# Last two experts: all rows summed, normed and stored without them, their lists' rows normed apart and written over

## The chip, the cores and the metric

The kernel runs on one core of one Trainium2 chip. A core has a matrix engine (PE), a vector engine (DVE), a scalar engine (ACT), GpSimd (POOL) and SyncE (SP), each with its own queue, worked off in order. SP, ACT and POOL also issue DMAs, which all run on the core's 16 DMA engines. The metric is the device time in microseconds of one execution, as the median of several runs.

## What is computed

One decoder block on 512 tokens of 1024 channels: a mixer (attention and a gated delta rule), then a mixture of experts, then a norm of each row. The change touches the last two. In the words of the reference:

```python
logits = xt @ w_router + b_router
top_v, top_e = top_k(logits, 4)            # 4 of 32 experts for each token
gates = softmax(top_v)
yb = clamped_swiglu(xb @ w1[e] + b1[e]) @ w2[e] + b2[e]
y[token] += yb * gate                      # over a token's four experts
x = x + gate2 * y
out = x * rsqrt(mean(x * x) + 1e-6) * final_norm_w
```

w1 of one expert is 1024 x 2048 and w2 is 1024 x 1024, both float32: 8 MB and 4 MB, 384 MB for all 32.

## The kernel before

The experts are run in an order by their number of tokens; `ROOM` (line 34) says how many tokens the list of each place can hold: 128, 96, 64 or 32, and so on. A list of 64 is one round whose rows are halves of a token (partitions 0 to 63 hold channels 0 to 511, the others the rest); one of 32 is a round of quarters; 96 is one of each. What does not fit goes through the loop at line 1481, which makes no turn with these inputs.

The steps (lines 1376 to 1379) go u0, u1, d0, u2, d1, ..., u31, d30, d31. Step "u" (`up`, line 1166) multiplies a list's rows by w1 and applies the activation (lines 1185 to 1187: ACT and DVE); step "d" (`down`, line 1190) multiplies by w2. Weights come in tiles of 1 MB, eight for a "u" and four for a "d", by SP's queue (lines 817 and 820), issued up to three steps ahead, into 15 buffers used in turn: six of the pool `late`, two of `wp` and seven of `moe` (`rawx`, line 800). A tile's buffer is free when PE has read it.

The DRAM tensor `yd` holds the rows so far: it starts as the mixer's output, and each round but the last scales its result by gates (line 1211, DVE) and adds it to `yd` by an indirect DMA that accumulates (line 1212, POOL). Such a DMA waits until the one before it has landed. The rows of a list are read from `h2d` by an indirect DMA (line 1156, POOL).

At the end (expert place 31, 64 tokens), `residual` (line 1219) loads the four blocks of 128 rows of `yd` once place 30 has been added; `gates_by_expert` and `bias2` make every token's share of the second bias with PE. `add_rows` (line 1247) brings the last list's result to its tokens by products with a matrix of zeros and ones, adds it to the blocks, norms each block (Square with a sum on ACT, the power -0.5 on POOL at line 1284, a scaling on DVE at lines 1297, 1300 and 1303) and stores it by SP (line 1307).

The order of each engine's queue is made when the program is built, by a planner that takes what it holds to be ready, the earlier in the program first; `in_order` fixes it in places. A weight load of SP's also waits until the eighth load before it has landed.

Of the kernel before, what the change touches and what calls it, by code (L numbers as in the profile page):

```python
# [14 lines left out]
OP = mybir.AluOpType  # L15
# [15 lines left out]

ROOM = [128, 128, 64, 64, 96, 64, 64, 192, 32, 96, 32, 160, 64, 64, 128, 64, 128, 64, 96, 64, 96, 64, 96, 64, 96, 64, 96, 64,
        32, 96, 32, 64]
# [9 lines left out]
def tile_block(ctx: ExitStack, tc, x, c, w_ada, b_ada, norm1_w, w_in, conv_w, A_log, dt_bias, dn_norm_w,  # L45
# [750 lines left out]
    E, HB, NR = 32, 64, 6  # L796
    NL, NM = 6, 7
    seq = [0]

    def rawx():  # L800
# [235 lines left out]
    def accumulator():  # L1036
        AL.append(ps2.tile([P, 512], F32, name="acc", bufs=6))
        return AL[-1]
# [148 lines left out]
            V.scalar_tensor_tensor(ut, sg, GATE_MAX, ut, op0=OP.min, op1=OP.mult)  # L1187
            UT[key] = ut

    def down(keys, rounds, tiles, ix, go, between=lambda i: None, last=False, first=False):  # L1190

        as_ = [AT.pop(c) for c in keys]
        accs = [accumulator() for _ in rounds]
# [10 lines left out]
                between(i)  # L1204
        for q, ((g, _), py) in enumerate(zip(rounds, accs)):
            if last:
                add_rows(py, go[:, q:q + 1], ix[:, q:q + 1], first)
# [11 lines left out]
    def residual():  # L1219

        for name, pool in (("res", moe), ("out", late)):
            ts = [pool.tile([P, 2048], F32, name="raw", bufs=NM if pool is moe else NL) for _ in range(2)]
            RES[name] = [ts[b // 2][:, b % 2 * D:b % 2 * D + D] for b in range(NTB)]
        for b in range(NTB):
            nc.sync.dma_start(RES["res"][b], yd[b * P:(b + 1) * P, :])
        RES["p2"] = [accumulator() for _ in range(2)]
        for n in range(2):
            bias2(RES["p2"][n], 1, n)

    def gates_by_expert():  # L1230

        g4 = late.tile([P, 2048], F32, name="raw", bufs=NL)[:, :NTB * 3 * E].rearrange("p (b a e) -> p b a e", b=NTB, a=3)
        for b in range(NTB):
            G.tensor_copy(g4[:, b], gt[:, 0, b, None, :].to_broadcast([P, 3, E]))
        gT = moe.tile([P, 2048], F32R, name="raw", bufs=NM)[:96, :T]
        pt = flat(ps2.tile([P, 4, P], F32, name="tr", bufs=2))[:96]
        for b in range(NTB):
            PE.transpose(pt[:, b * P:b * P + P], g4[:, b].rearrange("p a e -> p (a e)"), ident)
        S.copy(gT, pt)
        V.tensor_tensor(gT[64:], pt[64:], gT[64:].bitcast(F32), op=OP.subtract)  # L1240
        RES["g"] = gT

    def bias2(pn, b, n):

        PE.matmul(pn, RES["g"][:, b * P:b * P + P], b2s[:96, n * 512:n * 512 + 512], start=True, stop=False)

    def add_rows(py, gcol, ix, first):
# [8 lines left out]
        y = moe.tile([P, D], F32, name="ylast", tag="big")  # L1256
        yh, yl = (moe.tile([P, 512], F32R, name=n, tag="y", bufs=3) for n in ("yh", "yl"))
        V.scalar_tensor_tensor(y[:, :512], py, gcol, gate2s[2], op0=OP.mult, op1=OP.mult)
        S.copy(yh, y[:, :512])
        V.tensor_tensor(yl, y[:, :512], yh.bitcast(F32), op=OP.subtract)  # L1260
        of = lambda t, n: t[n * HB:n * HB + HB]
        ones_of = lambda b, n: one[n * HB:n * HB + HB, b]

        if not first:
            RES["p2"] = [accumulator() for _ in range(3)]
        others = [a for a in AL[-6:] if all(a is not q for q in RES["p2"][:2])]
        acc = [[flat(ps2.tile([P, 4, P], F32, name="tr", bufs=2)) for _ in range(2)], RES["p2"][:2], others[:2], others[2:]]
        fx = moe.tile([P, 3, 2 * NTB], F32, name="fx")
        cut = [slice(n * 512, n * 512 + 512) for n in range(2)]
        if first:  # L1270
            for b in (0, 2, 3):
                for n in range(2):
                    bias2(acc[b][n], b, n)
        for n in range(2):
            PE.matmul(acc[0][n], ident, RES["res"][0][:, cut[n]], start=not first, stop=False)

        def rms(b, xs):

            n = len(xs)
            sq, ms, sc = (fx[:, i, 2 * b:2 * b + n] for i in range(3))  # L1280
            for i, x in enumerate(xs):
                S.activation(y[:, :D // n], x, AF.Square, accum_out=sq[:, i:i + 1])
                S.activation(ms[:, i:i + 1], sq[:, i:i + 1], AF.Identity, scale=1.0 / D, bias=ms[:, 0:1] if i else epsc)
            G.tensor_tensor(sc[:, 0:1], ms[:, n - 1:n], mhalf[:, :1], op=OP.pow)

        with in_order(PE, V, S, G):
            for b in (1, 2, 3, 0):
                for n in range(2):
                    PE.matmul(acc[b][n], ones_of(b, n), of(yh, n), start=(b > 0 and not first), stop=False)
                    PE.matmul(acc[b][n], ones_of(b, n), of(yl, n), start=False, stop=True)  # L1290
                for a in {1: (1,), 3: (2, 3)}.get(b, ()):
                    for n in range(2):
                        V.tensor_tensor(RES["res"][a][:, cut[n]], RES["res"][a][:, cut[n]], acc[a][n], op=OP.add)
                if b == 1:
                    G.tensor_tensor(RES["out"][1], RES["res"][1], fnw, op=OP.mult)
                    rms(1, [RES["res"][1]])
            V.tensor_scalar(RES["out"][1], RES["out"][1], fx[:, 2, 2:3], None, op0=OP.mult)
            for b in (2, 3):
                rms(b, [RES["res"][b]])
                V.scalar_tensor_tensor(RES["out"][b], RES["res"][b], fx[:, 2, 2 * b:2 * b + 1], fnw, op0=OP.mult, op1=OP.mult)  # L1300
            rms(0, acc[0])
            for n in range(2):
                V.scalar_tensor_tensor(RES["out"][0][:, cut[n]], acc[0][n], fx[:, 2, 0:1], fnw[:, cut[n]], op0=OP.mult,
                                       op1=OP.mult)
                S.copy(RES["res"][0][:, cut[n]], acc[0][n])
        for b in (1, 2, 3, 0):
            nc.sync.dma_start(out[b * P:(b + 1) * P, :], RES["out"][b])


    for i, c in enumerate(COLS[1]):  # L1310
# [81 lines left out]
    for s, (what, i) in enumerate(steps):  # L1392
        while ahead < min(len(steps), s + 4):
            w_, j = steps[ahead]
            which, w_all = (1, w1) if w_ == "u" else (2, w2)
            load(which, j, weights(w_all, j), after=None if j > 1 else idx[0:1, 0:1].bitcast(F32))
            ahead += 1
        if what == "u" or i == E - 1:
            while pending:
                pending.pop(0)()  # L1400
        if what == "d":
            if i == E - 2:
                gates_by_expert()
            c0, c1 = COLS[i][0], COLS[i][-1] + 1
            down(COLS[i], ROUNDS[i], W.pop((2, i)), idx[:, c0:c1], gate[:, c0:c1], lambda _: pending and pending.pop(0)(),
                 i == E - 1, i == E - 1)
            if i == E - 2:
                residual()
            continue
        up(COLS[i], ROUNDS[i], W.pop((1, i)), sel_of(i))  # L1410
        for c in COLS[i]:
            pending.append(turn(AT, UT, "a", c))
        if i == 0:
# [67 lines left out]
    with tc.For_i(0, nrounds, 1):  # L1481
# [8 lines left out]
        down(["o"], [(2, 0)], W.pop((2, "o")), ix, go, last=True)  # L1490


def tables():
# [39 lines left out]
```

## Time and profile before

| | us |
|---|---|
| median of 3 runs (lowest, highest) | 1479.51 (1478.02, 1483.98) |
| the profiled execution's own time | 1475.38 |
| its span, first to last instruction | 1473.6 |
| busy: PE, DVE, ACT, POOL | 1377.2, 442.5, 270.3, 231.0 |
| read from HBM | 467.67 MB |

The expert stage is about the last 1000 us. Times below are microseconds from the start of the span. In a line of the timeline the first number is the start, the second the length; "x8" merges eight instructions; in brackets stands how long the engine sat idle before, and what ended that.

### The profile page before, as it was taken

What the parts mean: (1) busy time and instruction counts of PE and PEld (TensorE: products, weight loads), DVE (VectorE), ACT (ScalarE), POOL (GpSimd) and SP (SyncE); (2) the same over time, 40 slices, a digit from 0 to 9 for tenths busy, and PEclk for the clock granted to TensorE, in tenths of its full rate; (3) what the DMA queues carried; (4) which work ended last, traced back from release to release, by engine and by line L of the source; (5) the groups of instructions that cost most, each with busy time, mean ns of one, the idle gap of its engine ahead of it and who ended that gap; (6) DMA issues with size and microseconds to landing.
All of it is one profiled execution on the core that took longest, in us unless ns stands there. A gap on an engine that the chain in (4) does not pass through costs nothing.

```text
span 1473.6 us, 21094 instructions
## 1 busy us (share of the span) xinstructions
PE 1377.2 (93%) x8278; PEld 653.4 (44%) x8278; DVE 442.5 (30%) x1127; ACT 270.3 (18%) x595; POOL 231.0 (16%) x222
## 2 busy tenths in 40 slices
PE   5999898999899999999999999999999999988784
PEld 4777777779843333343333333333333333322131
DVE  3586985666781120201020220000211000100002
ACT  5554213573320000001010100000100001000002
POOL 0324105012321111110120120101111111100012
PEclk9999999999999999999999999999999999998798
DMA  9445465002689899999999999999999999999993
GB/s 342 148 143 163 149 204 166 29 13 82 282 333 346 322 387 414 406 412 413 410 404 410 417 405 413 411 406 408 417 409 407 416 411 415 410 410 411 419 384 137
DMA packets 100629, 482.11 MB, mean 327 GB/s; under 512 B 13112, under 2 KB 33240, under 8 KB 51376
## 3 DMA queue, kind: packets, MB, share of 16 engines
q1 hardware_dynamic: 88384, 459.54, 77.8%
q0 software_dynamic: 10960, 19.02, 5.4%
q10 hardware_dynamic: 1184, 2.18, 0.4%
q8 instruction: 66, 1.08, 0.3%
q14 instruction: 35, 0.29, 0.1%
HBM read 467.67 MB, written 17.44 MB: 329 GB/s over the span
## 4 chain that ended last, share of the span: by engine, by line
PE 56%; DMA 29%; DVE 9%; ACT 2%; issue 1%; POOL 1%; SPq 0%; ACTq 0%; POOLq 0%; DVEq 0%
PE acc L1178 27%; DMA raw<-in_w 24%; PE acc L1201 13%; PE tr L1148 2%; DVE macc L356 2%; DMA raw<-in_w_ada 2%; DVE wL L145 2%; DVE cv L313 1%; PE acc L1049 1%; PE ps L706 1%; DMA raw<-in_w_out 1%; PE mm L875 1%; PE mm L873 1%; PE mm L874 1%; POOL sn L327 1%
## 5 line engine op out<-in xcount | busy, mean ns | idle before, releaser
L1178 PE MATMUL acc<-raw,xS 128*64 128x512 f32 (+1 forms) x2944 | 575.2, 608 | 18.4 <-DMA raw<-in_w 18.3
L1178 PEld LDWEIGHTS acc<-raw,xS 128*64 128x64 f32 (+1 forms) x2944 | 173.3, 130 | 395.5 <-issue 331.2
L1201 PE MATMUL acc<-raw,aS 128*64 128x512 f32 (+1 forms) x1952 | 325.9, 515 | 9.9 <-DMA raw<-in_w 9.9
L1186 DVE TENSOR_SCALAR ut<-acc 128x512 f32<-128x512 f32 (+1 forms) x48 | 28.4, 616 | 526.2 <-PE acc L1178 477.1
L1201 PEld LDWEIGHTS acc<-raw,aS 128*64 128x64 f32 (+1 forms) x1952 | 98.7, 126 | 175.3 <-issue 134.7
L1185 ACT ACTIVATE sg<-acc 128x512 f32<-128x512 f32 (+1 forms) x48 | 24.4, 538 | 667.6 <-PE acc L1178 667.6
L1212 POOL DMA_INDIRECT yd<-y,idx x47 | 74.6, 1587 | 418.0 <-DVE y L1211 271.0
L1211 DVE SCALAR_TENSOR_TENSOR y<-acc,gate,gate 128x512 f32<-128x512 f32 (+1 forms) x47 | 30.3, 674 | 297.4 <-PE acc L1201 297.4
L1156 POOL DMA_INDIRECT xg<-h2d,idx x46 | 48.7, 1060 | 438.2 <-PE tr L1148 398.2
L284 PE MATMUL mm<-hH,wH 128*128 128x512 f32 x144 | 57.9, 402 | 2.4 <-ACT cu L310 2.3
L285 PE MATMUL mm<-hL,wH 128*128 128x512 f32 x144 | 57.4, 399 | 0.0
L286 PE MATMUL mm<-hH,wL 128*128 128x512 f32 x144 | 57.3, 398 | 0.0
L1149 ACT COPY xS<-tr 128x512 f32<-128x512 f32 (+1 forms) x46 | 24.1, 525 | 147.7 <-PE tr L1148 147.7
L1149 ACT COPY aS<-tr 128x512 f32<-128x512 f32 (+1 forms) x48 | 25.3, 528 | 125.2 <-PE tr L1148 102.3
L356 DVE SCALAR_TENSOR_TENSOR macc<-raw,cond,macc 128x512 f32<-128x512 f32 x62 | 46.0, 762 | 6.8 <-DMA raw<-in_w_ada 6.6
L145 DVE TENSOR_TENSOR wL<-raw,wH 128x1024 fp32r<-128x1024 f32 (+1 forms) x32 | 42.3, 1337 | 18.6 <-ACT wH L144 18.5
L144 ACT CAST wH<-raw 128x1024 fp32r<-128x1024 f32 (+1 forms) x34 | 34.6, 1057 | 63.3 <-DMA raw<-in_w_in 28.6
L294 PE MATMUL mm<-wH,hH 128*128 128x256 f32 (+1 forms) x96 | 29.8, 311 | 10.7 <-DVE aqk L512 4.9
L1148 PEld LDWEIGHTS tr<-ident,ut 128*128 128x128 f32 x166 | 23.7, 207 | 34.2 <-issue 30.9
L1148 PE MATMUL tr<-ident,ut 128*128 128x128 f32 x166 | 32.9, 315 | 0.3 <-ACT xS L1149 0.3
L284 PEld LDWEIGHTS mm<-hH,wH 128*128 128x128 f32 x144 | 27.4, 190 | 10.1 <-ACT cu L310 4.4
L313 DVE SCALAR_TENSOR_TENSOR cv<-cu,cols,cv 128x509 f32<-128x509 f32 (+2 forms) x36 | 29.6, 823 | 5.3 <-ACT cu L310 4.9
(404 smaller groups left out, 1490.6 us busy)
## 6 DMA issues: line engine op xcount, KB each, us to landing
raw<-in_w SPq DMA_DIRECT2D x384, 1024.0 KB
raw<-in_w_ada SPq DMA_DIRECT2D x16, 1024.0 KB
raw<-in_w_in SPq DMA_DIRECT2D x12, 1024.0 KB
raw<-in_w_ada SPq DMA_DIRECT2D x16, 512.0 KB
raw<-in_w_out SPq DMA_DIRECT2D x4, 1024.0 KB
raw<-in_w_in SPq DMA_DIRECT2D x2, 1040.0 KB
xn<-in_x SPq DMA_DIRECT2D x4, 512.0 KB
x<-in_x SPq DMA_DIRECT2D x4, 512.0 KB
```

The costliest lines, as they stand in the source:

```text
L145: eng.tensor_tensor(wl[:, cs], t[:, cs], wh[:, cs].bitcast(F32), op=OP.subtract)
L284: PE.matmul(ps, wh[:, k, js], hH[:, k], start=(k == 0), stop=False)
L285: PE.matmul(ps, wh[:, k, js], hL[:, k], start=False, stop=False)
L286: PE.matmul(ps, wl[:, k, js], hH[:, k], start=False, stop=(k == KT - 1))
L313: V.scalar_tensor_tensor(t[:, d:], u[:, :T - d], w(j), t[:, d:], op0=OP.mult, op1=OP.add)
L356: V.scalar_tensor_tensor(t, rs, cond[:, k:k + 1], t, op0=OP.mult, op1=OP.add)
L1148: tc.keep_in_program_order(PE.transpose(pt[:, j], src[:, cs], ident))
L1149: S.copy(xs[:, :m], pt[:, :m])
L1156: G.indirect_dma_start(out=t, out_offset=None, in_=h2d.rearrange("t (h d) -> (t h) d", h=g), in_offset=bass.IndirectOffsetOnAxis(ap=ix, ax ...
L1178: PE.matmul(a[n * r:n * r + r].rearrange("p (a c) -> p a c", c=w), of_channels(x, k, r), m, start=False, stop=(k == KT - 1), skip_group_ch ...
L1201: PE.matmul(ac[n * r:n * r + r, :w], of_channels(x, k, r), t[:, j * D + n * w:j * D + n * w + w], start=(k == 0), stop=(k == KT - 1), skip ...
L1212: G.indirect_dma_start(out=yd.rearrange("t (h d) -> (t h) d", h=g), out_offset=bass.IndirectOffsetOnAxis(ap=ix[:, q:q + 1], axis=0), in_=y ...
```

## The change

Place 30 now holds 64 tokens as place 31 does, and place 27 to 29 hold 32, 96 and 32. When the tiles of d29 have been asked for (`places`), the six `late` buffers are taken for the end, and the last 16 weight tiles go round the other nine. After u30 (`shares_of_b2`), the shares of the second bias are made for all tokens, for the rows of the two last lists, and a matrix that says which rows the two lists share (`both`). After d29 (`sums`), POOL reads the two lists' rows and then the four blocks from `yd`, each block gets its bias, is normed and is stored by SP. d30 and d31 (`last_rows`) add their result to their list's rows, norm these and write them over the rows of `out` by indirect DMAs: that of place 30 waits for the four stores, that of place 31 for that of place 30. The loop's `add_rows` is kept in a form of its own for lists that overflow.

```diff
-ROOM = [..., 96, 64, 96, 64, 96, 64,
-        32, 96, 32, 64]
+ROOM = [..., 96, 64, 96, 64, 96, 32,
+        96, 32, 64, 64]
...
+        while LAST and s < NL:
+            s = seq[0] % (2 + NL + NM)
+            seq[0] += 1
...
+    def shares_of_b2():
...
+        for b in range(NTB):
+            PE.transpose(pt[:, b * P:b * P + P], g_of(b), ident)
+        S.copy(gR[:, :T], pt)
...
+        for i in range(2):
+            for b in range(NTB):
+                for n in range(2):
+                    PE.matmul(pl[:96, (2 * i + n) * HB:(2 * i + n + 1) * HB], g_of(b), oh[i][:, b, 0:HB],
+                              start=(i == b == n == 0), stop=False, skip_group_check=True)
...
+        for b in range(NTB):
+            for n in range(2):
+                pn = accumulator()
+                PE.matmul(pn, gR[:, b * P:b * P + P], b2s[:96, cut[n]], start=True, stop=True)
+                S.copy(RES["out"][b][:, cut[n]], pn)
+        for i in range(2):
+            for n in range(2):
+                pn = accumulator()
+                PE.matmul(pn, gR[:, T + i * P:T + i * P + P], b2s[:96, cut[n]], start=True, stop=True)
+                S.copy(half_of(RES["y"][i], n), half_of(pn, n))
...
+            S.dma_start(half_of(RES["fn"], i), final_norm_w[None, cut[i]].to_broadcast([HB, 512]))
+
+    def norm_block(b):
+
+        sq, ms, sc = (RES["fx"][:, 3 * b + i:3 * b + i + 1] for i in range(3))
+        S.activation(RES["out"][b], RES["res"][b], AF.Square, accum_out=sq)
+        V.tensor_scalar(ms, sq, 1.0 / D, EPS, op0=OP.mult, op1=OP.add)
+        G.tensor_tensor(sc, ms, mhalf[:, :1], op=OP.pow)
+        V.scalar_tensor_tensor(RES["out"][b], RES["res"][b], sc, fnw, op0=OP.mult, op1=OP.mult)
+        return nc.sync.dma_start(out[b * P:(b + 1) * P, :], RES["out"][b])
+
+    def sums():
+
+        for i, e in enumerate(LISTS):
+            G.indirect_dma_start(out=RES["row"][i], out_offset=None, in_=yd.rearrange("t (h d) -> (t h) d", h=2),
+                                 in_offset=bass.IndirectOffsetOnAxis(ap=idx[:, COLS[e][0]:COLS[e][0] + 1], axis=0),
+                                 bounds_check=2 * T - 1, oob_is_err=False)
+        for b in range(NTB):
+            G.dma_start(RES["res"][b], yd[b * P:(b + 1) * P, :])
+        for i in range(2):
+            V.tensor_tensor(RES["row"][i], RES["row"][i], RES["y"][i], op=OP.add)
+        RES["stores"] = []
+        for b in range(NTB):
+            V.tensor_tensor(RES["res"][b], RES["res"][b], RES["out"][b], op=OP.add)
+            RES["stores"].append(norm_block(b))
+
+    def last_rows(i):
+        def rows(py, gcol, ix):
...
+            V.scalar_tensor_tensor(y, py, gcol, gate2s[2], op0=OP.mult, op1=OP.mult)
+            V.tensor_tensor(row, y, row, op=OP.add)
+            junk = moe.tile([P, 512], F32, name="sg", bufs=2)
+            S.activation(junk, row, AF.Square, accum_out=sq)
+            if i == 0:
+
+                acc = accumulator()
+                PE.matmul(acc, RES["both"], y, start=True, stop=True)
+                V.tensor_tensor(RES["row"][1], RES["row"][1], acc, op=OP.add)
+            pq = flat(ps2.tile([P, 4, P], F32, name="tr", bufs=2))[:, 0:1]
+            PE.matmul(pq, RES["pair"], sq, start=True, stop=True)
+            V.tensor_scalar(ms, pq, 1.0 / D, EPS, op0=OP.mult, op1=OP.add)
+            G.tensor_tensor(sc, ms, mhalf[:, :1], op=OP.pow)
+            V.scalar_tensor_tensor(row, row, sc, RES["fn"], op0=OP.mult, op1=OP.mult)
+            w = G.indirect_dma_start(out=out.rearrange("t (h d) -> (t h) d", h=2),
...
+            for o in RES["stores"]:
+                tc.add_manual_dep(w.ins, o.ins.name,
...
+            RES["stores"] = [w]
```

## Rows read from the trace of the kernel before

**Rows 1.** The page's slices of the span (each of 36.8 us; busy tenths, then GB/s).
```profile
PE   5999898999899999999999999999999999988784
DMA  9445465002689899999999999999999999999993
GB/s 342 148 143 163 149 204 166 29 13 82 282 333 346 322 387 414 406 412 413 410 404 410 417 405 413 411 406 408 417 409 407 416 411 415 410 410 411 419 384 137
```

**Rows 2.** Busy time by window near the end: the window, its length, then busy us (and instructions) of PE, PEld, DVE, ACT and POOL, the granted clock, the DMA engines' mean busy share, GB/s.
```profile
1280.00:1320.00 40.00, 36.83 (x224) 11.72 (x220) 3.28 (x5) 2.57 (x6) 4.81 (x4) 1.00 1.02 417
1380.00:1400.00 20.00, 13.25 (x62) 2.12 (x64) 0.85 (x2) 0.38 (x1) 0.00 (x0) 0.67 1.02 415
...
1430.00:1432.00 2.00, 0.24 (x7) 0.00 (x0) 0.02 (x1) 0.00 (x0) 0.00 (x0) 1.00 0.99 400
1432.00:1434.00 2.00, 1.83 (x16) 0.61 (x16) 0.00 (x0) 0.00 (x0) 0.00 (x0) 0.57 0.57 242
...
1438.00:1440.00 2.00, 0.67 (x10) 0.30 (x2) 1.17 (x2) 0.58 (x1) 0.93 (x1) 1.00 0.29 123
...
1446.00:1448.00 2.00, 0.97 (x6) 0.20 (x4) 0.00 (x0) 0.00 (x0) 0.00 (x0) 1.00 0.04 13
...
1450.00:1452.00 2.00, 1.77 (x7) 0.98 (x6) 1.03 (x2) 0.62 (x1) 0.00 (x0) 1.00 1.02 414
...
1466.00:1468.00 2.00, 0.00 (x0) 0.00 (x0) 0.00 (x0) 0.00 (x0) 0.00 (x0) 0.50 0.12 47
```

**Rows 3.** The timeline: SP's last weight loads, and PE's work on the tiles of d31 as they land.
```profile
1408.06 18.87 SPq L820 DMA_DIRECT2D raw<-in_w  x8
...
1444.64 1.94 PE L1201 MATMUL acc<-raw,aS 128*64 128x512 f32 x8 [0.63 <-DMA raw<-in_w]
...
1447.60 1.94 PE L1201 MATMUL acc<-raw,aS 128*64 128x512 f32 x8 [1.02 <-DMA raw<-in_w]
```

**Rows 4.** The chain of work that ended last: its pieces between the last accumulation into `yd` and the first sum.
```profile
1439.07 8.22 DMA yd<-y,idx
...
1448.76 5.88 DMA raw<-yd
1454.63 0.69 DVE raw L1293
```

**Rows 5.** The timeline after the last product: scaling, norm and stores.
```profile
1449.59 0.75 DVE L1258 SCALAR_TENSOR_TENSOR ylast<-acc,gate,gate 128x512 f32<-128x512 f32 x1 [10.07 <-PE acc L1201]
1455.39 1.06 ACT L1282 ACTIVATE ylast<-raw 128x1024 f32<-128x1024 f32 x1 [4.41 <-DVE raw L1293]
1459.16 5.27 SPq L1307 DMA_DIRECT2D out<-raw  x4
1459.51 0.58 ACT L1282 ACTIVATE ylast<-tr 128x512 f32<-128x512 f32 x1
1459.99 0.19 ACT L1282 ACTIVATION_READ_ACCUMULATOR ylast<-tr 128x1 f32 x1
1460.93 1.28 DVE L1300 SCALAR_TENSOR_TENSOR raw<-raw,fx,fnw 128x1024 f32<-128x1024 f32 x1 [0.44 <-POOL fx L1284]
1461.49 1.14 POOL L1284 TENSOR_TENSOR fx<-fx,mhalf 128x1 f32<-128x1 f32 x1 [0.59 <-ACT fx L1283]
```

**Rows 6.** The end of the span by the lines of the loop's entry (1481) and of the program's end (1529): an instruction of an engine's queue, its count, shortest, median and longest ns, and where the first and the last start.
```profile
L1481 SPq EVENT_SEMAPHORE  x21: 17/27/28, 1464.7 to 1468.5; - x21
...
L1529 POOLq DRAIN  x3: 46/103/4726, 1468.0 to 1473.3; - x3
```

**Rows 7.** DMAs that POOL issues: the instruction on POOL (ns as in group 6) and, under it, the time from its start to the landing: line 1212's accumulations, line 1156's gathers in the last 374 us, line 1358's load of 512 KB (start 438.7); then three issues of the mixer's time from the page of DMA issues (count, KB each, median us to landing).
```profile
L1212 POOL DMA_INDIRECT yd<-y,idx x47: 1552/1584/1647, 501.5 to 1439.1; - x47
...
DMA to landing us min/median/max: 8.2/8.9/10.4
...
L1156 POOL DMA_INDIRECT xg<-h2d,idx x10: 1037/1072/1076, 1121.1 to 1307.4; - x10
...
DMA to landing us min/median/max: 5.9/7.0/7.1
...
L1358 POOL DMA_DIRECT2D fnw<-in_final_norm_w x1: 605/605/605, 438.7 to 438.7; - x1
...
DMA to landing us min/median/max: 9.2/9.2/9.2
...
X<-da POOLq DMA_DIRECT2D x2, 256.0 KB, 5.7
...
dx<-blk POOLq DMA_DIRECT2D x2, 128.0 KB, 5.0
...
db<-X POOLq DMA_DIRECT2D x1, 8.0 KB, 1.6
```

**Rows 8.** The work on the second bias and copies out of PE's sums, by timeline and (the last) by line.
```profile
1436.12 0.64 PE L1238 MATMUL tr<-ident,raw 128*96 128x128 f32 x4
...
1450.03 1.08 PE L1245 MATMUL acc<-b2s,raw 96*128 96x512 f32 x4
...
L1149 ACT COPY aS<-tr x4: 372/479/586, 1372.7 to 1437.3; 128x512 f32<-128x512 f32 x2, 128x256 f32<-128x256 f32 x2
```

**Rows 9.** The timeline: DVE's two operations that end u31.
```profile
1428.50 0.69 DVE L1186 TENSOR_SCALAR ut<-acc 128x512 f32<-128x512 f32 x1 [14.44 <-PE acc L1178]
...
1429.31 0.71 DVE L1187 SCALAR_TENSOR_TENSOR ut<-sg,ut 128x512 f32<-128x512 f32 x1
```

More of the change, by code (lines that the diff above doesn't have):

```diff
@@ L798, in tile_block @@
     seq = [0]
+    LAST = []
     def rawx():
@@ L1188, in up, with down @@
             UT[key] = ut
-    def down(keys, rounds, tiles, ix, go, between=lambda i: None, last=False, first=False):
+    def down(keys, rounds, tiles, ix, go, between=lambda i: None, last=None):
         as_ = [AT.pop(c) for c in keys]
@@ L1206, in down @@
             if last:
-                add_rows(py, go[:, q:q + 1], ix[:, q:q + 1], first)
+                last(py, go[:, q:q + 1], ix[:, q:q + 1])
                 continue
@@ L1230, in gates_by_expert, with places @@
[L1230 to L1235, printed above, removed]
+    LISTS = (E - 2, E - 1)
+    cut = [slice(n * 512, n * 512 + 512) for n in range(2)]
+    half_of = lambda t, n: t[n * HB:n * HB + HB]
+    def places():
+        a, c = (late.tile([P, 2048], F32, name="raw", bufs=NL) for _ in range(2))
+        for name in ("out", "res"):
+            ts = [late.tile([P, 2048], F32, name="raw", bufs=NL) for _ in range(2)]
+            RES[name] = [ts[b // 2][:, b % 2 * D:b % 2 * D + D] for b in range(NTB)]
+        RES["y"] = [a[:, n * 512:n * 512 + 512] for n in range(2)]
+        RES["g"] = a[:, 1024:1408].rearrange("p (b a e) -> p b a e", b=NTB, a=3)
+        RES["row"], RES["fn"] = [a[:, 1408:1920], c[:, 0:512]], c[:, 512:1024]
+        RES["oh"] = [c[:, o:o + n].rearrange("p (b r) -> p b r", b=NTB) for o, n in ((1024, 512), (1536, 256))]
+        RES["both"], RES["pair"], RES["fx"] = c[:, 1792:1920], c[:, 1920:2048], a[:, 1920:1936]
+        LAST.append(1)
@@ L1236, in gates_by_expert @@
         pt = flat(ps2.tile([P, 4, P], F32, name="tr", bufs=2))[:96]
         for b in range(NTB):
[L1238 to L1247, printed above, removed]
+            PE.transpose(pt[:, b * P:b * P + P], g_of(b), ident)
@@ new lines, in shares_of_b2 @@
+        S.copy(gR[:, :T], pt)
+        V.tensor_tensor(gR[64:, :T], pt[64:], gR[64:, :T].bitcast(F32), op=OP.subtract)
+        pl = flat(ps2.tile([P, 4, P], F32, name="tr", bufs=2))
+        for i in range(2):
[4 more added lines that the diff above has]
+        for b in range(NTB):
+            PE.matmul(pl[:, 2 * P:2 * P + HB], oh[0][:, b], oh[1][:, b], start=False, stop=(b == NTB - 1), skip_group_check=True)
@@ new lines, in shares_of_b2 @@
+        for i in range(2):
+            for n in range(2):
+                pn = accumulator()
+                PE.matmul(pn, gR[:, T + i * P:T + i * P + P], b2s[:96, cut[n]], start=True, stop=True)
+                S.copy(half_of(RES["y"][i], n), half_of(pn, n))
+            V.memset(RES["row"][i], 0.0)
+            V.tensor_tensor(RES["pair"][:, i * HB:i * HB + HB], ident[:, 0:HB], ident[:, HB:P], op=OP.add)
+            S.dma_start(half_of(RES["fn"], i), final_norm_w[None, cut[i]].to_broadcast([HB, 512]))
@@ new lines, in norm_block @@
+    def norm_block(b):
[6 more added lines that the diff above has]
+    def sums():
+        for i, e in enumerate(LISTS):
+            G.indirect_dma_start(out=RES["row"][i], out_offset=None, in_=yd.rearrange("t (h d) -> (t h) d", h=2),
[6 more added lines that the diff above has]
+        RES["stores"] = []
+        for b in range(NTB):
+            V.tensor_tensor(RES["res"][b], RES["res"][b], RES["out"][b], op=OP.add)
+            RES["stores"].append(norm_block(b))
@@ new lines, in last_rows @@
+    def last_rows(i):
+        def rows(py, gcol, ix):
+            y, row = RES["y"][i], RES["row"][i]
+            sq, ms, sc = (RES["fx"][:, 12 + j:13 + j] for j in range(3))
+            V.scalar_tensor_tensor(y, py, gcol, gate2s[2], op0=OP.mult, op1=OP.mult)
[12 more added lines that the diff above has]
+            w = G.indirect_dma_start(out=out.rearrange("t (h d) -> (t h) d", h=2),
+                                     out_offset=bass.IndirectOffsetOnAxis(ap=ix, axis=0), in_=row, in_offset=None,
+                                     bounds_check=2 * T - 1, oob_is_err=False)
+            for o in RES["stores"]:
+                tc.add_manual_dep(w.ins, o.ins.name,
+                                  mybir.DependencyInfo(mybir.DependencyClass.Sync, mybir.DependencyReason.DATA),
+                                  reason="the same rows")
+            RES["stores"] = [w]
+            RES["ix"] = RES.get("ix", []) + [ix]
+        return rows
@@ L1264, in add_rows @@
[L1264 to L1301, printed above, removed]
-            for n in range(2):
-                V.scalar_tensor_tensor(RES["out"][0][:, cut[n]], acc[0][n], fx[:, 2, 0:1], fnw[:, cut[n]], op0=OP.mult,
-                                       op1=OP.mult)
-                S.copy(RES["res"][0][:, cut[n]], acc[0][n])
@@ L1306, in add_rows @@
-        for b in (1, 2, 3, 0):
-            nc.sync.dma_start(out[b * P:(b + 1) * P, :], RES["out"][b])
+        S.copy(yh, y)
+        V.tensor_tensor(yl, y, yh.bitcast(F32), op=OP.subtract)
+        for b in range(NTB):
+            for n in range(2):
+                acc = accumulator()
+                o = half_of(one, n)[:, b]
+                PE.matmul(acc, o, half_of(yh, n), start=True, stop=False)
+                PE.matmul(acc, o, half_of(yl, n), start=False, stop=True)
+                V.tensor_tensor(RES["res"][b][:, cut[n]], RES["res"][b][:, cut[n]], acc, op=OP.add)
@@ L1310, in tile_block, with other_rows @@
+    def other_rows(py, gcol, ix):
+        for y, i in zip(RES["y"], RES["ix"]):
+            add_rows(y, i)
+            V.memset(y, 0.0)
+        y = moe.tile([P, D], F32, name="ylast", tag="big")[:, :512]
+        V.scalar_tensor_tensor(y, py, gcol, gate2s[2], op0=OP.mult, op1=OP.mult)
+        add_rows(y, ix)
+        for b in range(NTB):
+            norm_block(b)
     for i, c in enumerate(COLS[1]):
@@ L1489, in tile_block @@
         AT["o"] = transposed(UT.pop("o"), "a", 2)
-        down(["o"], [(2, 0)], W.pop((2, "o")), ix, go, last=True)
+        down(["o"], [(2, 0)], W.pop((2, "o")), ix, go, last=other_rows)
 def tables():
```

37 lines of the change are left out of this document (18 added, 19 removed).

## Prediction

> **What bounds the kernel now.** First the page's slices: from about the sixteenth on, the DMA engines' digit is 9 and the rate stays between 404 and 419 GB/s up to the last but one slice [rows 1]. The reader is to see there that the expert stage is a stream of weights: a tile of 1 MB (1.049 million bytes) each 2.55 us at 411 GB/s. Then the windows near the end: PE is busy for 36.83 of 40 us in one stage and 13.25 of 20 in another while the DMA share stays at 1.02 [rows 2]; PE waits, the stream does not. The same view shows the stream's end: from 1432 on the share falls to 0.57, 0.29 and 0.04. Some of the 16 engines have finished their part, others go on until the last tile is used at 1447.60 [rows 3]. SP issued d31's last load by 1426.93, some 20.7 us, or eight tiles' time, before that.
>
> Then the chain of waits, for what comes after: the last accumulation into `yd` lands at 1447.29, the four blocks are read until 1454.63, and the sums start [rows 4]; norms and stores follow, the last store being issued by 1464.43 [rows 5]. POOL's long drain begins at 1468.0, which I take as the landing of the last store, and the span ends at 1473.6, 5.6 us later [rows 6]. So 26.0 us lie between the last tile and the end, and the change can only work on these, and on what it puts ahead of them.
>
> **What it moves into the stream.** The blocks' reads leave the tail and lie beside weights, in a stage whose DMA share is 1.0. Bytes: 4 x 512 KB of blocks, 2.10 million, at the 414 GB/s at which the same reads ran [rows 2] are 5.1 us; two gathers of at most 128 x 2 KB, 0.52 million, are 1.3; two loads of 64 x 2 KB of the final norm, 0.26 million, are 0.6; one accumulation of 64 rows falls away, 0.26 million bytes written, -0.6. Sum 6.3 us, by which the last tile comes later: 1453.9. Bounds: 0 if all of it fits into the engines' idle time after 1432, and 7.0 if nothing falls away. I take 6.3, because in the stage in which the reads must run the share is 0.99 to 1.02 [rows 2], and because at the end tiles still come one per 2.5 to 3 us (1444.64, 1447.60 [rows 3]) while most engines stand idle: the last engines set the pace, and each transfer gives them their part too.
>
> The Trainium skill says in "DMA: Bandwidth & Descriptors", "Issuing engines are not separate DMA queues", that DMAs of the scalar, sync and gpsimd engines run on the same 16 engines and interleave, so that another issuer saves issue time only. By that rule the reads gain nothing by POOL's queue. Here the rate with gathers and accumulations beside the stream stays at 417 GB/s [rows 2], which fits; no row shows a large read from POOL in this stage.
>
> **The tail after.** The four stores are behind the last weights on SP's queue. Where their data are ready by then, they need 5.1 us on the last engines and land, as before's last store did (moving until about 1466.3 [rows 2], landed 1468.0), 1.7 later: 1453.9 + 5.1 + 1.7 = 1460.7. Place 30's write waits for all four. On POOL, behind this waiting instruction, stand the power for place 31 (1.14 us) and its write, which also waits until the first has landed. A plain indirect write is nowhere in the trace. From above: the accumulations, 8.9 us [rows 7], beside a full stream and with a read of what they add to. From below: a direct DMA of POOL in a quiet time, 1.6 for 8 KB. Nearest are 5.0 and 5.7 for 128 and 256 KB; I take 5.0 from start to landing, since the queue is empty then. Two in a row: 1465.7, 1470.7. With 5.6 to the end: 1476.3, so +2.7 us on 1473.6.
>
> By the fit in the Trainium skill's "DMA: Bandwidth & Descriptors", "Anatomy of one DMA — SWDGE (gpsimd) path" (2.0 us and the bytes at 436 GB/s) such a write of 256 KB would be 2.6 us, an estimate that no run here shows; with POOL's 1.58 us ahead of it the two writes would be 1.6 us shorter together, 1474.7.
>
> Place 31's own way is not the late one: last tile 1453.9, its products 1.94, then scaling 0.75, row's sum 0.69, square 0.58 + 0.19, the pair's product about 0.5, the mean about 0.3, power 1.14, scaling 0.75 [rows 5, 9], and some 0.7 of handing over: ready at 1461.4, 4.3 us before it may be written.
>
> **What costs nothing, and by which cover.** The shares: on PE four transposes (0.64), 20 small products (at 0.16 as the transposes, 3.2) and 12 of 96x512 (0.36 each, 4.3), 8.1 us [rows 8]; on ACT twelve copies and one more of 512 columns, 0.59 each, 7.7 us, and a smaller one. From u30's end to the last tile 20 tiles of d29 to d31 pass; each leaves PE 2.55 - 1.94 = 0.6 us, 12 us in all. Without this cover PE would end up to 8 us late. Nine buffers instead of 15: eight loads are under way at most, so the ninth has just to be read when the next is asked for; where PE lags by more than a tile, fewer are under way, but the last engines still have work until it lags by seven. With the cover gone each tile would pay about 2 us of start. The order of `ROOM` changes no product: the 96-row place comes one place earlier, and its two rounds' writes to `yd` are done before d29. Sums and norms of the blocks are 4 x (1.28 + 1.28) us on DVE, which is busy 3.28 us of 40 in such a stage [rows 2].
>
> **Rivals.**
> *Slower: place 31 waits behind the blocks on DVE and ACT.* Both work in order, and `sums` stands ahead of u31 in the program; if the planner held the reads for quicker than u31, the blocks' sums and squares are queued ahead of u31's activation. d29's last tile lands 16 tiles before the end, 1413.1; PE is done at 1415 to 1423 (with the shares ahead of it), the accumulation starts 1 us later and lands 8.9 later, 1425 to 1433 [rows 7]; two gathers and four reads take POOL 2 x 1.07 + 4 x 0.6 = 4.5, and a read of 512 KB beside the stream landed after 9.2. Alone that is 1438.7 for the last block; sharing half the engines' rate with the stream, 2.6 million bytes take 12.7 and with the 6.7 that the 9.2 hold beyond 2.5 it is 1453 at worst. Call that R. Place 31 then starts at R + 5.2 (the last block's norm) + 1.4 + 1.4 (transposes, copy), needs 7.8 for four tiles and 5.6 to its write: R + 21.4. From R = 1444.3 on this decides; at 1451 the end is 1451 + 21.4 + 5.0 + 5.6 = 1483.0, +9.4, 1488.9 by the median. For it: every number of that chain is longer than in a quiet machine. Against: half of R's span costs nothing or little. Chance 0.18.
>
> *Slower: the writes cost what accumulations cost*, 8.9 each: 1460.7 + 17.8 + 5.6 = 1484.1, +10.5, 1490.0. Against: they read nothing of `out`, and no stream runs beside. Chance 0.11.
>
> *The change doesn't do what it says: the blocks come after the last tile.* R over 1453.9 brings before's tail back, with two writes more: 1473.6 + 10.0 = 1483.6, 1489.5. It needs PE to lag some 10 us more than I find. Chance 0.04.
>
> *Faster: the reads fill what is idle.* The last tile stays at 1447.60 and the stores are through by then: 1.94 + 5.6 + 5.0 + 5.6 behind it, 1465.7, -7.9, 1471.6. For it: between 1432 and 1448 most engines' time is idle. Against: the tiles' pace there. Chance 0.07.
>
> **How the numbers follow.** The forecast has 0.60: +2.7 us, no change that a measurement tells (0.5%, 7.4 us). Added to the profiled execution's own 1475.38 it gives 1478.1; that one stands 4.1 below the median of the runs, so on 1479.51 it is 1482.2, and I say 1482. Its own range, by writes of 4.2 to 6 and a last tile 5 to 7 later, is 1479 to 1486. With the slower cases from 1488.9 to 1490.0, the range is 1475 to 1491. Below 1475 lies only the faster rival. Faster by over 0.5%: 0.07; slower: the three cases, 0.33, less a little for those that stay under 7.4 us and more for what the forecast can lose, 0.32; within: 0.61.
>
> **What would show it.** The last tile used some 6 us later (about 1454) with the DMA share at 1.0 up to 1438; stores landing 5 to 7 us behind it; the wait of place 30's write put down to a store and that of place 31's to place 30's; 4 to 6 us each. Wrong: a last tile near 1448; an activation of u31 that starts long after its products; SP's last loads behind a store in its queue, which would hold the stream up.

## The result and the profile after

The changed kernel takes 1497.25 us (median of 5 runs, 1493.73 to 1502.82), the kernel before 1483.98 (median of 5, 1478.02 to 1486.27). The ratio is 1.0112, 95% interval 1.0089 to 1.0135: 16.6 us slower, where 1482 was forecast and 1491 was the end of the range. (The two medians alone are 13.3 us apart, which is the lower end of that interval; the text goes by the ratios.)

One reading aid for all traces here: the start of the expert stage differs by up to 11 us from one profiled execution to the next, so traces are set against each other from SP's first load of an expert's weights. It starts at 366.40 in the trace of before and at 376.59 in that of after. From it to the end of the span are 1107.2 us before (1473.6 - 366.4) and 1124.4 after (1501.0 - 376.6): 17.2 us more, which agrees with the ratio. (The profiled execution after is the slowest of the five, 1502.82, 5.6 above their median.)

The slices of the page after, under those of [rows 1]:

```profile
PE   5998889999999999999999999999999999897934
DMA  9445565002779899999999999999999999999990
GB/s 337 145 146 157 166 195 173 1 1 84 285 309 354 315 383 414 407 412 410 412 406 411 417 400 417 406 415 407 414 408 409 416 412 407 416 411 412 370 385 23
```

The stream is the same until the last slices, which are windowed here as in [rows 2]:

```profile
1410.00:1440.00 30.00, 26.65 (x186) 12.22 (x185) 5.08 (x18) 7.89 (x16) 5.90 (x7) 1.00 1.02 402
...
1445.00:1450.00 5.00, 0.32 (x2) 0.00 (x0) 1.51 (x2) 1.15 (x2) 0.00 (x0) 0.93 1.01 415
1450.00:1455.00 5.00, 0.00 (x0) 0.00 (x0) 3.87 (x6) 1.35 (x3) 1.13 (x2) 0.50 1.02 418
...
1465.00:1470.00 5.00, 5.00 (x14) 1.39 (x14) 0.00 (x0) 0.46 (x1) 0.00 (x0) 0.52 0.07 27
1470.00:1475.00 5.00, 4.14 (x18) 1.06 (x14) 1.81 (x3) 0.72 (x2) 0.00 (x0) 1.00 0.00 0
1475.00:1480.00 5.00, 5.00 (x24) 1.79 (x24) 1.22 (x3) 0.00 (x0) 0.55 (x1) 1.00 0.00 0
```

From 1450 to 1455 the DMA engines are full and PE does nothing; from 1465 on it is the other way round. In before's windows, and in [rows 3], PE waited for the stream's last tiles; here the stream is over and PE has work left. The timeline of PE says what it stood for:

```profile
1439.95 1.94 PE L1182 MATMUL acc<-raw,xS 128*64 128x512 f32 x8 [0.94 <-DMA raw<-in_w]
1443.38 1.94 PE L1205 MATMUL acc<-raw,aS 128*64 128x512 f32 x8 [1.49 <-DMA raw<-in_w]
1463.74 1.10 PE L1152 MATMUL tr<-ident,ut 128*128 128x128 f32 x4 [18.42 <-DVE ut L1191]
1464.77 7.84 PE L1205 MATMUL acc<-raw,aS 128*64 128x512 f32 x24
1473.46 1.13 PE L1319 MATMUL acc<-raw 128*128 128x512 f32 x2 [0.85 <-DVE raw L1312]
...
1475.83 7.08 PE L1205 MATMUL acc<-raw,aS 128*64 128x512 f32 x30
```

The first line is the end of u31, the second the first tile of d30. Then PE stands 18.42 us, put down to DVE's line 1191, the second operation of u31's activation. It does so inside d30: the four transposes of place 31's rows (line 1152) stand in PE's queue between d30's first and second tile, since `down` calls a pending `turn` after each of its first three tiles. So seven tiles (24 and 32 products) come after the stall, not four. What DVE did meanwhile, where [rows 9] had u31's activation right behind its products:

```profile
1445.95 1.23 DVE L1304 TENSOR_TENSOR raw<-raw 128x1024 f32<-128x1024 f32 x1 [3.00 <-DMA raw<-yd]
...
1456.94 1.23 DVE L1304 TENSOR_TENSOR raw<-raw 128x1024 f32<-128x1024 f32 x1 [1.04 <-DMA raw<-yd]
...
1460.91 1.28 DVE L1289 SCALAR_TENSOR_TENSOR raw<-raw,fnw 128x1024 f32<-128x1024 f32 x1 [0.66 <-POOL raw L1288]
1462.11 0.68 DVE L1190 TENSOR_SCALAR ut<-acc 128x512 f32<-128x512 f32 x1
1462.90 0.69 DVE L1191 SCALAR_TENSOR_TENSOR ut<-sg,ut 128x512 f32<-128x512 f32 x1
```

u31's products end at 1441.9. DVE could have taken them up then; it waits for the reads of the blocks instead (the releaser in the first two lines), and the activation comes 20.2 us later, behind the scaling of the last block. ACT's queue has the same order: its part of the activation follows right behind the square of the last block (1458.26).

```profile
1459.32 0.58 ACT L1189 ACTIVATE sg<-acc 128x512 f32<-128x512 f32 x1
```

It is the wait of the first rival, on both engines. POOL's timeline has the rest of the end:

```profile
1476.18 0.55 POOL L1324 TENSOR_TENSOR raw<-raw,mhalf 128x1 f32<-128x1 f32 x1 [15.31 <-DVE raw L1323]
1486.02 0.55 POOL L1324 TENSOR_TENSOR raw<-raw,mhalf 128x1 f32<-128x1 f32 x1 [9.29 <-DVE raw L1323]
1486.97 1.34 POOL L1326 DMA_INDIRECT out<-raw,idx  x1 [0.40 <-issue]
1491.27 1.01 POOL L1326 DMA_INDIRECT out<-raw,idx  x1 [2.96 <-DMA out<-raw,idx]
```

Place 30's rows were scaled by 1477.5 (DVE, line 1325, 1476.76 and 0.75 long), and the stores were through: the DMA share is 0.00 from 1470. Yet its write starts at 1486.97, because place 31's power (the second line) stands ahead of it in POOL's queue, and that needs place 31's last product. So both writes come after everything else, in a row; the chain of waits ends with them, where [rows 4] had the accumulation and the reads. Its last DMA is place 30's write:

```profile
1486.97 3.51 DMA out<-raw,idx
```

### The profile page after: what moved, and what is told of

It is laid out like the page before. It is cut to its first block, busy times and chain, and to the rows that moved or that the text cites. A ratio compares the mean times of both kernels' runs of the same rounds, so it can differ in the third digit from the quotient of the medians.

```text
span 1501.0 us, 21193 instructions
## 1 busy us (share of the span) xinstructions
PE 1389.3 (93%) x8308; PEld 664.1 (44%) x8308; DVE 451.3 (30%) x1146; ACT 275.3 (18%) x602; POOL 232.6 (15%) x226
```

## The experiments

The theory: three orders in in-order queues, made by the planner, cost the 16.6 us; above all the blocks ahead of u31's activation on DVE. The main rival: bytes and writes cost more than forecast. In the table, "from first load" is the span's end counted from SP's first expert load, and "last tile" the start of d31's last products, counted in the same way where the trace shows that tile on its own. Both are from one trace each: e6, e7 and e8 have the same stream of loads, and their last tiles spread over 2.9 us, so a difference of 2 or 3 us between two rows is not shown by these columns alone.

| kernel | ratio to before (95%) | from first load | last tile |
|---|---|---|---|
| before | 1 | 1107.2 | 1081.2 |
| after | 1.0112 (1.0089, 1.0135) | 1124.4 | |
| e1_ut_first | 1.0056 (1.0027, 1.0085) | 1117.7 | |
| e2_write_first | 1.0101 (1.0069, 1.0134) | 1120.7 | |
| e9_blocks_first | 1.0089 (1.0061, 1.0118) | 1119.3 | |
| e3_all_orders | 0.9990 (0.9973, 1.0006) | 1107.2 | 1086.9 |
| e6_norm_row_by_pool | 1.0006 (0.9982, 1.0031) | 1108.7 | 1088.6 |
| e7_free_writes | 1.0009 (0.9990, 1.0028) | 1106.5 | 1085.8 |
| e8_one_write | 0.9989 (0.9964, 1.0014) | 1106.3 | 1088.7 |
| e4_no_block_reads | 0.9972 (0.9948, 0.9996) | 1102.2 | 1082.9 |
| e5_room_only | 1.0018 (0.9990, 1.0046) | 1107.0 | |

### u31's activation ahead of the blocks

```diff
-            V.tensor_tensor(RES["res"][b], RES["res"][b], RES["out"][b], op=OP.add)
+            behind(V.tensor_tensor(RES["res"][b], RES["res"][b], RES["out"][b], op=OP.add).ins, ut)
```

(`ut` is the instruction of line 1191 for u31; the lists' rows' sums get the same. The run also moves these sums and the blocks' norms in the program from behind d29 to behind u31, so that ACT's squares no longer stand ahead of u31 either.)

> One edit: on DVE the sums of the lists' rows and of the four blocks are queued behind u31's activation. Theory (the order of DVE's queue holds u31's activation back until the last block is normed, and PE stands 18.4 us in d30 for it): that stall goes, u31's activation ends within 2 us of its products; PE does d30 beside the reads and then stands at the product for rows that both lists hold, which waits for place 30's scaling behind the last norm, so d31 starts some 11 us earlier than in the changed kernel: 5 to 7 us slower than before instead of 16.6. Rival (the bytes of the blocks' reads and of the stores in the stream set the end, the stall only shows it): the end moves by less than 4 us, 12 us or more slower than before.

Measured: +8.3 us by the ratio (0.0056 of the 1481.5 that before took there; 4.0 to 12.6 by its interval), so that half of what the change had lost comes back; from the first load it is +10.5. That lies between the theory's 5 to 7 and the rival's 12, and d31 starts 8.1 us earlier than in the change, not 11. PE's timeline has the two steps of the theory, d30's tiles beside the reads and then the next stall:

```profile
1438.98 1.94 PE L1207 MATMUL acc<-raw,aS 128*64 128x512 f32 x8 [1.46 <-DMA raw<-in_w]
...
1450.19 1.94 PE L1207 MATMUL acc<-raw,aS 128*64 128x512 f32 x8 [1.84 <-DMA raw<-in_w]
1459.74 2.08 PE L1324 MATMUL acc<-raw 128*128 128x512 f32 x2 [7.62 <-DVE raw L1317]
```

The product with `both` (line 1324) stands in PE's queue ahead of d31's tiles, and waits for place 30's scaling, which stands behind the blocks on DVE: one wait was taken away and the next in the same queue showed.

### Place 31's power behind place 30's write

```diff
-            G.tensor_tensor(sc, ms, mhalf[:, :1], op=OP.pow)
+            pw = G.tensor_tensor(sc, ms, mhalf[:, :1], op=OP.pow)
+            if i:
+                behind(pw.ins, RES["stores"][0].ins.name)
```

> One edit: on POOL the power for place 31 is queued behind place 30's write. Theory (that write is ready at about 1477.6 in the changed kernel's trace and issued at 1487.0, because POOL's queue has place 31's power ahead of it): it is issued some 9 us earlier, lies beside d31, and place 31's write follows its own row at once, 3.9 us earlier: 12 to 14 us slower than before. Rival (place 30's write waits for the stores): no change, 16 to 17 us slower.

By time this is inconclusive: 15.0 us slower than before by the ratio, where 12 to 14 were expected, and its interval (10.2 to 19.9) holds the rival's 16 to 17 as well. The trace shows the step: place 30's write is issued beside d31, as POOL's timeline says, and the end from the first load is 3.7 us earlier (1120.7 against 1124.4), which is about the 3.51 that the first write took. Within the trace it is seen too: place 31's write starts 44.1 us behind the first products of d30 (1435.23), and 47.9 behind them in the change's trace.

```profile
1469.50 1.07 POOL L1328 DMA_INDIRECT out<-raw,idx  x1 [1.08 <-DVE raw L1327]
...
1479.37 1.06 POOL L1328 DMA_INDIRECT out<-raw,idx  x1 [1.08 <-DVEq L1544]
```

### All orders, and the one order alone

e3 has both edits, puts the product with `both` and the norms' products behind d31's last product on PE, interleaves the blocks' sums with their scalings, and keeps the small values of place 31's norm in columns of their own.

```diff
+            if i == 1:
+                acc = accumulator()
+                behind(PE.matmul(acc, RES["both"], RES["y"][0], start=True, stop=True).ins, RES["mm"].ins.name)
+                RES["finish"](acc)
```

> All orders at once: the sums behind u31's activation on DVE, each block's sum behind the scaling of the second before it, PE's three small products of the lists' rows behind d31's last product, place 31's power behind place 30's write. Theory (the queues' orders cost what lies between the forecast and the measurement, some 14 us): PE has no wait but for weights until d31's end, and the end is set by the stores, place 30's write and place 31's: 0 to 5 us slower than before, the forecast being 2.7. Rival (bytes): 9 us or more slower, with the last tile landing over 10 us later than in the kernel before.

Measured: no difference from before that can be told. The whole loss of the change is gone with the same loads, reads and writes, so the orders made it. PE now waits for nothing but weights, in its timeline:

```profile
1435.10 1.94 PE L1207 MATMUL acc<-raw,aS 128*64 128x512 f32 x8 [1.64 <-DMA raw<-in_w]
1438.78 1.94 PE L1207 MATMUL acc<-raw,aS 128*64 128x512 f32 x8 [1.07 <-DMA raw<-in_w]
1442.56 1.94 PE L1207 MATMUL acc<-raw,aS 128*64 128x512 f32 x8 [1.84 <-DMA raw<-in_w]
...
1456.80 1.94 PE L1207 MATMUL acc<-raw,aS 128*64 128x512 f32 x8 [0.65 <-DMA raw<-in_w]
```

Its two writes, in POOL's timeline:

```profile
1462.73 1.07 POOL L1336 DMA_INDIRECT out<-raw,idx  x1 [1.08 <-DVE raw L1331]
...
1467.25 1.06 POOL L1336 DMA_INDIRECT out<-raw,idx  x1 [2.83 <-DMA out<-raw,idx]
```

e9 is e3 with one order turned back: the blocks are again ahead of u31's activation, by taking the sums' `behind` edges out (with the interleaving) and calling them before u31.

> e3 with the blocks' sums and scalings put ahead of list 31's activation on DVE and ACT again, as in the changed kernel; the other two orders of e3 stay (both's product behind the last down projection, list 30's write ahead of list 31's power). Theory, that this one order is most of the 16.6 us: TensorE stands some 18 us inside list 30's down projection, seven tiles follow it, the end is 10 to 13 us later than in e3, about 1.007 of the kernel before. The rival, that the three orders only cost in a row together: within 4 us of e3.

Measured: 1.0089 where about 1.007 was expected (0.0099, or 14.6 us, above e3's ratio), and 12.1 us more than e3 from the first load (10 to 13 expected). PE's timeline has the stall back, at nearly the same length and with the same releaser:

```profile
1433.18 1.94 PE L1207 MATMUL acc<-raw,aS 128*64 128x512 f32 x8 [1.47 <-DMA raw<-in_w]
1453.16 1.10 PE L1152 MATMUL tr<-ident,ut 128*128 128x128 f32 x4 [18.05 <-DVE ut L1191]
1454.20 13.18 PE L1207 MATMUL acc<-raw,aS 128*64 128x512 f32 x56
```

So of the 17.2 us between the traces of e3 and of the change, 12.1 are this one order, and 5.1 are the other two on top of it, with the clock in them: in this trace the granted clock, 0.50 while PE stood, is at 0.93 some three microseconds after PE has resumed (1456 to 1457), and the 56 products behind the stall took 13.18 us; in after's it stayed at half for most of 24 products, which cost some 2.2 us (an estimate: 7.84 - 24 x 0.236, by the 7.08 for 30).

### What the reads cost

e4 is e3 without the four reads; the blocks' sums take the shares of the second bias alone.

```diff
-        for b in range(NTB):
-            G.dma_start(RES["res"][b], yd[b * P:(b + 1) * P, :])
```

> e1 to e3's orders without the four reads of the blocks' sums (the blocks' values are left out: their scaling takes the bias share alone, so the stored rows lack y). It measures what 2 MB of reads cost the stream of the last weights. My theory, that the bytes are priced in full on the last loads: without them the tiles of the last two down projections come every 2.5 us and not every 3.7, the last tile about 5 us earlier than in e3 measured from SP's first expert load, the end about 5 us earlier too, so about 0.995 of the kernel before. The rival, that the reads fill time in which the DMA engines stand idle: the end within 1.5 us of e3.

Measured: the last tile 4.0 us earlier than in e3 and the end 5.0 earlier, both from the first load; the ratios differ by 0.0018, 2.7 us, in the same direction, but the intervals overlap. PE's timeline has the tiles 2.3 to 2.6 us apart where e3's came every 3.7:

```profile
1437.14 1.94 PE L1207 MATMUL acc<-raw,aS 128*64 128x512 f32 x8 [0.82 <-DMA raw<-in_w]
1439.69 1.94 PE L1207 MATMUL acc<-raw,aS 128*64 128x512 f32 x8
1442.02 1.94 PE L1207 MATMUL acc<-raw,aS 128*64 128x512 f32 x8 [0.40 <-DMA raw<-in_w]
1444.49 1.94 PE L1207 MATMUL acc<-raw,aS 128*64 128x512 f32 x8 [0.54 <-DMA raw<-in_w]
```

So by the traces the reads do not fill idle time: 4.0 of their 5.1 us by bytes are paid for on the last tiles. The times agree in direction and leave the size open.

### A hole in the stream, and what it costs

In every trace in which ACT issues the final norm's loads (the change, e1 to e4 and e9), SP's loads falter once, some 80 to 100 us ahead of the end. My reading: in the program a load's landing is counted on one of eight semaphores, which the loads of SP's and ACT's queues take in turn; the two loads of the final norm on ACT's queue stand between SP's in that count, so that SP's next load waits for one that lies six back and not eight. SP's waits in after's trace (in all, how many, the longest) have both sides of it, SP waiting for the final norm's loads and the one long wait for weights:

```profile
SPq L824 <- DMA raw<-in_w: 164.9, 81, 7.0
...
SPq L821 <- DMA raw<-in_final_norm_w: 3.6, 2, 2.1
```

In e3 the wait is 7.0 us as well, and the load that waited starts at 1389.48, 19.95 us behind the load six back (1369.53); the load ahead of it starts at 1381.93, 19.84 behind the one eight back (1362.09). ACT issues its two loads only at 1399.43: it is their place in the count that held SP, not their bytes. e5 is the kernel before with the new `ROOM` alone, to see whether the order of the places makes the hole:

```diff
-ROOM = [..., 96, 64, 96, 64,
-        32, 96, 32, 64]
+ROOM = [..., 96, 64, 96, 32,
+        96, 32, 64, 64]
```

> The kernel before with the changed kernel's ROOM and nothing else: the 96-row place one earlier, place 30 with 64 rows. Theory: no change beyond 0.2% (3 us), the stream sets the pace either way. Rival (the gap in SP's loads near 1396 to 1408 of the changed kernel's trace, some 4 us of the stream, comes from the new order of the places): 3 to 5 us slower, with such a gap in the trace.

It made no difference that can be told and no hole. e6 is e3 with the two loads issued by POOL:

```diff
-            S.dma_start(half_of(RES["fn"], i), final_norm_w[None, cut[i]].to_broadcast([HB, 512]))
+            G.dma_start(half_of(RES["fn"], i), final_norm_w[None, cut[i]].to_broadcast([HB, 512]))
```

> e3 with the two final-norm loads issued by POOL and not by ACT. Theory of the hole: an ACT load takes one of the eight lanes that SP's loads take in turn, so SP waits for a load six back; without it no 7.0 us wait at SP's third load of list 29's down projection, no stretch below 340 GB/s between 1385 and 1410, the last tile 1 to 3 us earlier from SP's first expert load, and the time 1 to 3 us below e3 (0.997 to 0.999). The rival, that the hole only empties engines that make the time good afterwards: the hole is gone and the time is within 1 us of e3.

The windows of e3 and, below, of e6 (columns as in [rows 2]):

```profile
1385.00:1390.00 5.00, 5.00 (x26) 2.86 (x24) 0.00 (x0) 0.00 (x0) 0.26 (x1) 1.00 0.90 324
1390.00:1395.00 5.00, 3.38 (x16) 0.84 (x12) 0.73 (x4) 0.00 (x0) 1.55 (x1) 1.00 0.92 298
```

```profile
1385.00:1390.00 5.00, 5.00 (x26) 3.20 (x24) 0.00 (x0) 0.00 (x0) 0.00 (x0) 1.00 1.03 382
1390.00:1395.00 5.00, 4.19 (x21) 1.40 (x17) 0.73 (x4) 0.00 (x0) 2.14 (x3) 1.00 1.03 408
```

The share is back at 1.0 and the longest wait at line 824 down to 3.5 us:

```profile
SPq L824 <- DMA raw<-in_w: 164.2, 83, 3.5
```

So the cause of the hole is right. (Not all of the expectation came true: from 1400 to 1404 the rate is 300 GB/s, at a share of 1.01.) Its price was not found: the last tile is not earlier than in e3 (1088.6 against 1086.9), and the ratio is 1.0006 against 0.9990. That favours the rival, that the stream makes the hole good before its end; a price of 1 or 2 us is less than these runs can tell.

### What the two writes in a row cost

e7 was to free place 31's write from place 30's: rows that both lists hold get an index beyond the bound in place 30's write, and the wait between the two is taken out of `last_rows`.

```diff
+        V.scalar_tensor_tensor(in_both[:, 2:3], in_both[:, 0:1], 4096.0, in_both[:, 1:2], op0=OP.mult, op1=OP.add)
+        V.tensor_copy(own, in_both[:, 2:3])
...
-                RES["stores"] = [w]
```

> e6, and the rows that both lists hold get an index beyond the bound in list 30's write, so that it skips them; then the two writes share no row and list 31's waits for the four stores alone. Theory: the 3.7 us from the first write's start to its landing go from the end, so 3 to 4 us below e6, 5 to 7 us below the kernel before (about 0.9955). The rival: list 31's write then stands behind something else, its power on POOL or the first write's issue, and the time is within 1 us of e6.

It did not test this. POOL's timeline still has a wait for the first write, although the explicit one is out; I take it that the build of the program orders two writes to one tensor by itself, which no run here shows. The edit also lost e3's order on POOL: place 30's write is again behind place 31's power (1466.38).

```profile
1467.35 1.33 POOL L1343 DMA_INDIRECT out<-raw,own  x1 [0.42 <-issue]
1471.26 1.01 POOL L1343 DMA_INDIRECT out<-raw,idx  x1 [2.58 <-DMA out<-raw,own]
```

e8 prices it another way: it is e6 without place 30's write.

```diff
+                if i == 0:
+                    return
                 w = G.indirect_dma_start(out=out.rearrange("t (h d) -> (t h) d", h=2),
```

> e6 without the write of list 30's rows (they are left as the four block stores wrote them, so 128 rows of the output lack the last two experts' share in them). It prices what e7 was meant to price: list 31's write then waits for the four stores and its own rows alone. Theory: the first write's 3.7 us from start to landing, with the 0.5 us behind it, go from the end: 3.5 to 4.5 us below e6, about 0.9975 of the kernel before. The rival, that list 31's rows or the stores are as late as the first write's landing: within 1.5 us of e6.

The remaining write starts 7.6 us behind the last tile (1462.54 - 1454.94), in e6 10.3 (1464.78 - 1454.46): 2.7 us, between the two expectations. The ratio is 0.0017 below that of e6, 2.5 us, within the intervals. Place 31's own rows are scaled by 1462.25 (DVE, line 1335, 1461.50 and 0.75), so with one write gone they are what is late; the two writes in a row are worth some 2.7 us by these traces, not 3.7. The last write in e8 and, below, in e6:

```profile
1462.54 1.09 POOL L1338 DMA_INDIRECT out<-raw,idx  x1 [1.08 <-DVEq L1561]
```

```profile
1464.78 1.06 POOL L1336 DMA_INDIRECT out<-raw,idx  x1 [2.69 <-DMA out<-raw,idx]
```

## Why the prediction was wrong

**The step that failed** is the sentence "Place 31's own way is not the late one", together with the price of the first rival. I took u31's activation to follow its products, and gave the other order 0.18. It was the order that the program had: the activation came 20.2 us behind its products, and e9 shows that order to be worth 12.1 us by itself.

**The rival's working was too low as well, which made its chance too small.** R, the last block's read, was put between 1438.7 and 1453 on before's clock. The sum that waits for it started at 1456.94; less the 10.2 us by which the expert stage began later, that is 1446.7, the middle of it. But I let place 31 need R + 21.4 to its write, "7.8 for four tiles". Measured, its row was scaled 30.4 us behind R (1486.61 + 0.75 - 1456.94). Three things were missing. Seven tiles wait, not four (18.1 us from 1464.8 to 1482.9, where the sum had 7.8), for the transposes stand inside d30; that could have been read in `down`, whose `between` is called after its first three tiles. The first three of them ran mostly at half clock: PE had stood 18 us, and the granted clock was 0.50 to 0.52, the 1.2 GHz level, until 1470. And the product with `both` stood in PE's queue ahead of d31. In my sum place 31's rows may be written from 1465.7 on; with 30.4 in the place of 21.4 the rival decides from R = 1465.7 - 30.4 = 1435.3 and not from 1444.3; that lies below all of R's span. Once that order is in the queues, no R that I thought possible would have hidden it. With R = 1446.7 and 30.4 the rival's own sum gives 1446.7 + 30.4 + 5.0 + 5.6 = 1487.7, 14.1 us behind before's end; the traces have 17.2, and POOL's order, below, is about the rest.

**POOL's order was not priced.** I named place 31's power as queued behind place 30's write. It was ahead of it, so that the two writes could only start after place 31's last product. That is the 3.7 us between e2's trace and after's, and 3.8 (47.9 - 44.1) counted within them.

**What moves into the stream: right.** Forecast 6.3 us on the last tile; e3, where nothing but weights holds PE, has 5.7 (1086.9 - 1081.2), e6 to e8, built on it, have 4.6 to 7.5, and without the reads it is 1.7. The Trainium skill's "DMA: Bandwidth & Descriptors", "Issuing engines are not separate DMA queues", says that work of another engine's queue shares the same 16 engines. e4 agrees with 4.0 us on the last tile for 5.1 us of bytes, and so does e6, where another issuer changed no time that can be told.

**The tail: right once the orders are.** Forecast 22.4 us from the last tile to the end (1453.9 to 1476.3); e3 has 20.3 (1456.80 to 1477.1). The stores were through by 1461, where the DMA share falls from 0.06 to 0.01, 4.2 us behind the last tile and not 6.8, and place 30's write waited for DVE and not for them (in e3 its norm stands behind d31's last product). Two writes in a row at 5.0 each were 4.5 from start to start in e3 and 3.71 from start to landing. From the second write's start the end is 9.9 us away, forecast 10.6. Place 31's rows were ready 7.3 us behind the last tile in e8, forecast 7.5. By the fit in the Trainium skill's "DMA: Bandwidth & Descriptors", "Anatomy of one DMA — SWDGE (gpsimd) path", such a write would be 2.6 us, an estimate. The runs show 3.1 to 3.7 from start to landing, and 1.8 to 2.6 less POOL's 1.0 to 1.3 us of issuing.

**"Nine buffers ... at nothing" and 0.6 us for the final norm's loads.** The loads' bytes were all that I counted; through the shared counting of landings they did open a hole. e6 shows that it costs no time that can be told, so that the nothing stands, by luck and not by the cover that I named.

**The other covers held.** The shares of the second bias lie on PE and ACT between u30 and the last tile, and in e3 PE waits for weights all the same; the order of `ROOM` costs nothing that can be told (e5).

**Why even the good order gains nothing.** 5.7 us later at the last tile and 5.7 us shorter behind it (26.0 to 20.3): the tail's reads are moved, not hidden, and what the tail saves the stream pays. To gain, bytes have to go, as e4 shows, but those bytes are the blocks. Behind the last tile, where the DMA engines idle, is where before has them.

## What to carry to other kernels

When work that waits for a DMA is put ahead of other work in the program, ask of each in-order queue which waiting instruction now stands in front of which ready one, and follow the one that is held up through every queue it feeds: here a sum on DVE held an activation, this held transposes on PE, and these held three tiles of another expert. Price such a rival by the queue that is really there, down to the calls in between; then look where it decides, before giving it a chance. And moving a transfer beside a stream that sets the pace moves its price with it.

## What the runs showed of the hardware

A read of 512 KB by POOL took a median of 16.3 us from issue to landing beside the weight stream in after's trace (11.5 in e6's), where a load of the same size had taken 9.2 in [rows 7]; while the four reads ran, a 1 MB tile came every 3.7 us at a DMA share of 1.0. A hole that left the DMA engines at 226 GB/s for four microseconds (1388 to 1392 in e3's trace) cost nothing that can be told at the stream's end some 60 us later: e6, which lacks it, takes no less (1.0006 against 0.9990). And the clock: each stall of 18 us on PE brought the granted clock to 0.50, the 1.2 GHz level, and so did e1's stall of 7.6 us. After PE had resumed it rose in some 3 us in one trace (e9, 1453.2 to 1456) and in some 6 us in two others (after, 1463.7 to 1469.6; e2, 1455.3 to 1461.5), so that a wait on TensorE costs its own length and a part of the work behind it that I could not have given beforehand.
